# Attention stage: norm factors broadcast later in the first pair, value products of two units side by side in odd steps

## The chip, the cores and the metric

The kernel runs on one core of a Trainium2 chip. The metric is the device time of one execution in microseconds (us), lower is better. A core has TensorE (PE, matrix products, with its weight loads shown as PEld), VectorE (DVE), ScalarE (ACT), GpSimd (POOL) and SyncE (SP, which issues DMAs here). Each engine works through its own queue in order; semaphores tie them together.

## The reference

A decoder trunk of two layers on one sequence of 1024 positions and width 1024. Layer 0 mixes with an RG-LRU recurrence, layer 1 with stick-breaking attention; each is followed by a SwiGLU network. The change lies in the attention of layer 1, cut here to what matters (16 heads of 64; `hn` is the normed input):

```python
hn = rms_norm(h, mix_norm[1])
q, k, v = split(hn @ w_qkv)                 # 16 heads of 64 each
for blk in range(8):                        # 128 queries at a time
    z = (q_blk @ k[:t1].T) * scale
    strict = s_idx < t_idx
    log_fail = where(strict, log_sigmoid(-z), 0)
    suffix = reverse_cumsum(log_fail) - log_fail
    weights = where(strict, exp(log_sigmoid(z) + suffix), 0)
    out_blk = weights @ v[:t1]
h = h + concat(out_blks) @ w_o
```

## The kernel before

Products in nearly full precision are made from a high and a low part of each operand, three matmuls per product (`mm3`, lines 143 to 145), in f32 form with 512 columns. The value products (`av_part`, line 1802) are f16.

**Attention works on pairs of heads.** There are 8 pairs. Each pair needs its Q, K and V projections: `qkv_steps` makes them one after the other (`which` 0, 1, 2), each for two halves `n` of the positions, each half being 8 calls of `mm3`, one per call of the generator. So a half is 8 calls and a pair 48. After the eighth call of a half comes `evacuate`, in two parts: the first in the same call, the second at the start of the next call, before that call's products.

- Q: first part, ACT copies the rounded high part (L1660). Second part, DVE subtracts for the low part (L1651) and stages `spread` (ACT copies, L1648, and DMAs).
- K: first part, DVE multiplies the projection by the norm factors (L1665). Second part stages `high`, ACT's rounding copy (L1673), which stages `low` (DVE's subtraction, then `place`, ACT copies L1640 and DMAs), which stages the rest of `place`.
- V: first part, DVE scales (L1610); second part, DVE takes differences (L1612) and stages an ACT copy two steps later (L1627), then DVE's low part and transposing DMAs.

`stage` puts a task on a list; `due` runs it at the start of the next step (or a later one), ahead of everything else in that step. A second list, `later`, gives up one task per step: the splitting of the next projection's weights (`whi` on ACT, L1558, `wlo` on DVE, L1559), the squares of the weights (ACT, L1553), the column sums of these (PE, `n_ps`, L1537, followed by DVE at L1543) and the collecting of finished heads (`gather`, `add_v`, `parts`).

**The step loop.** One step `u` takes one chunk of scores and one unit of value products. Both lists have 192 entries, 24 per pair; the chunk is ten steps ahead of the unit. In a step the code issues, in this order: the staged tasks; loads of stored rows back to the chip; the scores (`z_part`, PE, L1690 and L1691, into one of two PSUM buffers that `n_ps` also uses), their sigmoid (ACT, L1728) and the scan (DVE, L1735 or L1738); for the chunk of the step before, ACT's cast (L1750), DVE's low part (L1751) and a transposing DMA; in even steps the value products of unit `u`; one task of `later`; two calls of the projections (`fill`); in odd steps the value products of unit `u`. In the last pair the weights are transposed on PE instead (`t_part`, `t_split`): even steps do this for the units `u+2` and `u+3`, after the value products of unit `u`.

The order written here is the order on each engine (`manual_schedule`), so an instruction that waits holds up all that stand behind it on its engine.

**The start.** 42 calls of the first pair's projections run before the step loop, numbered `i`. A table `between` puts other work after a call: `stats` (PE sums of squares, then the square root on ACT and small DVE operations that make the norm factors `rcol`) and `broadcast_r` (PE spreads the factors over all partitions, L192, and DVE copies them to `rbc`, L199). Call 17 begins the K projection, calls 24 and 32 end its halves, which read `rbc[0]` and `rbc[1]`. The column sums of the first pair come in call 22.

Of the kernel before, what the change touches and what calls it, by code (L numbers as in the profile page):

```python
# [34 lines left out]
def trunk(  # L35
# [152 lines left out]
    def broadcast_r(ps_pool, tag, n):  # L188
        ps = ps_pool.tile([P, NB], F32, tag=tag, name="rb_ps")
        for i in range(4):  # L190
            b = 4 * n + i
            nc.tensor.matmul(  # L192
                ps[:, i * P : (i + 1) * P],
                lhsT=rcol[:, b : b + 1].broadcast_to([P, P]),
                rhs=ident,
                start=True,
                stop=True,
            )
        nc.vector.tensor_copy(rbc[n], ps)  # L199
# [1288 lines left out]
    with ExitStack() as st:  # L1488
# [5 lines left out]
        psO = st.enter_context(tc.tile_pool(name="psO", bufs=2, space=PSUM, reuse_waits="tile"))  # L1494
# [25 lines left out]
        def stage(task, steps=1):  # L1520
            soon.append([steps, task])

        def load_link(i):
            q, which = divmod(i, 3)
            if q < NP:
                raws[i] = load_raw(cols(w_qkv, which * D + q * P), (ND,))
            else:
                mix[0].load(which)
# [233 lines left out]
        def unit_list(q, hx):  # L1762
            kbs = ((0, 1, 2, 3), (4, 5, 6, 7, 0, 1, 2, 3))
            return [(q, hx, G, kb, kb == 4 * G, kb == 3) for G in range(2) for kb in kbs[G]]
# [20 lines left out]
        def av_part(q, hx, G, kb, first, last):  # L1785
            q0 = (max(kb, 4 * G) - 4 * G) * P
            if first:
                av[0] = psO.tile([P, NB], F32, tag="o", name="av_ps")
            ps = av[0]
            k = kb % 4  # L1790
            parts_ = []
            if q == LAST:
                parts_ = [(q0, NB, t[:, q0:].rearrange("p (j c) -> p j c", c=P)) for t in ready.pop((hx, G, kb))]
            else:
                T_ = T[q, hx, G, kb // 4 == G]
                if kb // 4 == G and k < 2:
                    tp = T[q, hx, G, "pair"]
                    parts_ = [(q0, 2 * P, tp[:, x : x + 3 : 2] if k == 0 else tp[:, 4 + x : 5 + x]) for x in range(2)]
                c0 = max(q0, 2 * P) if kb // 4 == G else 0
                parts_ += [(c0, NB, T_[:, 2 * k + x, max(k - 2, 0) * (kb // 4 == G) :]) for x in range(2)]  # L1800
            for i, (c0, c1, t) in enumerate(parts_):
                nc.tensor.matmul(  # L1802
                    ps[:, c0:c1].rearrange("p (j c) -> p j c", c=P), lhsT=VV[q][:, hx, kb], rhs=t,
                    start=first and i == 0, stop=last and i == len(parts_) - 1,
                )
            if not last:
                return
            a, b = (top, bot)[:: 1 if hx == 0 else -1]

            def gather():  # L1810
                if hx == 0:
                    oo[q, G] = ap.tile([P, NB], F32, tag="oo", name="oo", bufs=2)
                o = oo[q, G]
                nc.scalar.copy(o[a], ps[b])
                nc.vector.tensor_add(o[a], ps[a], o[a])

            def add_v():
                eng = nc.vector if q == NP - 1 else nc.gpsimd
                eng.tensor_add(oo[q, G], oo[q, G], VT[q][:, G * NB + 1 : (G + 1) * NB + 1])

            def parts():
                o = oo[q, G]
                down = f32(av_[q])

                def both(hi, lo):
                    nc.scalar.activation(hi, o, AF.Copy, scale=down)
                    nc.vector.scalar_tensor_tensor(lo, o, down, f32(hi), op0=ALU.mult, op1=ALU.subtract)

                if not kept(q, G):
                    both(xh[q][G], xl[q][G])  # L1830
                else:
                    oh = ap.tile([P, NB], F32R, tag="oh", name="oh", bufs=1)
                    both(oh, o.bitcast(F32R))

                    def store():
                        nc.sync.dma_start(od[q, G][0], f32(oh))
                        nc.sync.dma_start(od[q, G][1], o)

                    stage(store)

            later.insert(0, gather)
            if hx == 1:
                later.extend((add_v, lambda: None, parts))
# [3 lines left out]
        units = [u for q, hx in heads for u in unit_list(q, hx)]  # L1847
# [27 lines left out]
        with tc.manual_schedule(engines={E.PE, E.Activation, E.DVE, E.Pool, E.SP}):  # L1875


            load_link(1)
            first = qkv_steps(0)
            between = {  # L1880
                12: lambda: stats(rbc[0], psO, "o", 0),
                16: lambda: stats(rbc[1], psO, "o", 1),
                17: lambda: broadcast_r(psO, "o", 0),
                18: lambda: nc.gpsimd.tensor_scalar_mul(rs, rcol, -SC),
                21: lambda: broadcast_r(psO, "o", 1),
            }
            def due():
                now = soon[:]
                soon.clear()
                for steps, task in now:  # L1890
                    if steps > 1:
                        stage(task, steps - 1)
                    else:
                        task()

            for i in range(1, 2 * ND * NH + 3 + AHEAD):
                next(first)
                if i in between:
                    between[i]()
                due()  # L1900
                if i > 4 and later:
                    later.pop(0)()

            gains = [len(units) - x for x in (31, 29, 27)]

            last_two, out_work = len(units) - 2 * 12, out_fill()
            amount = {x: 2 for x in (9, 10, 11, 12)}
            amount.update({x: 1 for x in (*range(-5, 1), *range(14, 21))})
            c = 0

            def turn(some):
                for a in some:
                    turn_weights(*a)

            for u in range(-LEAD, len(units)):
                some = chunks[c : c + 1]
                c += 1
                if u < -2:
                    for _ in range(2):
                        next(fill, None)  # L1920
                due()
                for _ in range(2 if u >= last_two - 8 and u % 2 == 0 else 1):
                    if back:
                        nc.sync.dma_start(*back.pop(0))
                for a in some:
                    z_rest(z_part(*a), *a)
                if u % 2 == 0 and u + 2 >= last_two:
                    av_part(*units[u])
                    two = [(x, t_part(*x)) for x in units[u + 2 : u + 4]]
                    for x, tp in two:  # L1930
                        ready[x[1:4]] = t_split(tp, *x)
                for a in some:
                    scan(*a)
                now, turning = turning, list(some)
                turn(now)
                if u % 2 == 0 and 0 <= u < last_two - 2:
                    av_part(*units[u])
                if u - last_two == 9:
                    mix[0].w[mix[0].order[1]] = next_weights(mix[0].raw.pop(1), nc.gpsimd)
                if later:  # L1940
                    later.pop(0)()
                if u >= -2:
                    for _ in range(2):
                        next(fill, None)
                for _ in range(amount.get(u - last_two, 0)):
                    next(out_work)
                if u in gains:
                    z_rest(z_part(*chunks[c]), *chunks[c])
                    scan(*chunks[c])
                    turning.append(chunks[c])  # L1950
                    c += 1
                if u % 2 and u >= 0:
                    av_part(*units[u])
            while later or soon:
                due()
                if later:
                    later.pop(0)()
# [46 lines left out]
```

## Time and profile before

| what | us |
|---|---|
| median of 3 runs | 2117.93 (2116.54 to 2119.25) |
| the profiled execution | 2116.7 |
| its span | 2114.9 |
| PE busy | 2096.8 |
| DVE busy | 1771.3 |
| ACT busy | 1184.5 |

The engine table gives busy time over the whole span, the windows give it for a stretch, with the granted TensorE clock (1.00 is full speed). A row of a timeline has the start, the duration, the engine, the line, the operation with what it writes and reads, a count, and in brackets the idle time before it with what ended that. The duration of a matmul reaches over its pipeline, so the distance of two starts tells what it costs the queue. The attention stage lies between about 953 and 1400 us of the span.

### The profile page before, as it was taken

The page shows a single profiled execution, that of the slowest core. Times are in us where ns is not written, and L with a number is a line of the kernel's source. Part 1 is how long each engine was busy: PE and PEld are TensorE (multiplying, and loading weights), DVE is VectorE, ACT ScalarE, POOL GpSimd, SP SyncE. Part 2 cuts the span into 40 slices and gives each one's busy share as a digit, 9 for nine tenths or more (in the row PEclk, how much of TensorE's full clock was granted, in tenths as well). Part 3 has the DMA queues.
Part 4 walks back from the last instruction along what each step waited for, and adds up shares of the span by engine and source line. Part 5 has one row for each costly group of instructions (what it writes and reads, how often), then busy time and mean ns, then how long its engine had stood idle before and what let it go on. Part 6 is the DMA issues. An engine that isn't in the chain of part 4 may idle for free.

```text
span 2114.9 us, 27976 instructions
## 1 busy us (share of the span) xinstructions
PE 2096.8 (99%) x10022; PEld 1719.9 (81%) x10022; DVE 1771.3 (84%) x2579; ACT 1184.5 (56%) x1906; POOL 139.1 (7%) x118
## 2 busy tenths in 40 slices
PE   8999999999999999999999999999999999999998
PEld 7888888888888888887777777678888888888887
DVE  7888778888888788796999999967888888888886
ACT  6567535444344445466878878744544444454456
POOL 1222010000000000000011111012000000000002
PEclk9999999999999999999999999999999999999999
DMA  7111431334444776533888898942224444686452
GB/s 240 50 50 40 149 100 55 105 124 145 161 133 152 256 251 190 152 118 91 162 179 175 177 178 174 247 170 80 85 90 150 140 150 155 202 269 225 126 153 90
DMA packets 446444, 313.89 MB, mean 148 GB/s; under 512 B 166104, under 2 KB 361824, under 8 KB 446304
## 3 DMA queue, kind: packets, MB, share of 16 engines
q1 hardware_dynamic: 446144, 311.84, 51.1%
q8 instruction: 78, 1.28, 0.3%
q14 instruction: 62, 0.51, 0.1%
q10 hardware_dynamic: 160, 0.27, 0.0%
HBM read 183.57 MB, written 82.84 MB: 126 GB/s over the span
## 4 chain that ended last, share of the span: by engine, by line
PE 93%; DVE 3%; ACT 1%; DMA 1%; issue 1%; SPq 0%; DVEq 0%; ACTq 0%
PE p_ps L143 18%; PE p_ps L145 18%; PE p_ps L144 18%; PE qk_ps L143 3%; PE qk_ps L145 3%; PE qk_ps L144 3%; PE a_ps L144 3%; PE a_ps L145 3%; PE a_ps L143 3%; PE ob_ps L143 3%; PE ob_ps L145 3%; PE ob_ps L144 3%; PE av_ps L1802 2%; PE i_ps L145 1%; PE i_ps L144 1%; PE i_ps L143 1%
## 5 line engine op out<-in xcount | busy, mean ns | idle before, releaser
L143 PE MATMUL p_ps<-vh,wbh 128*128 128x512 f32 x524 | 204.9, 391 | 0.0
L144 PE MATMUL p_ps<-vl,wbh 128*128 128x512 f32 x524 | 204.5, 390 | 0.0
L145 PE MATMUL p_ps<-vh,wbl 128*128 128x512 f32 x524 | 204.0, 389 | 0.2 <-DVE wbl L726 0.2
L143 PE MATMUL p_ps<-vh,wch 128*128 128x512 f32 x524 | 204.2, 390 | 0.0
L145 PE MATMUL p_ps<-vh,wcl 128*128 128x512 f32 x524 | 204.1, 389 | 0.0
L144 PE MATMUL p_ps<-vl,wch 128*128 128x512 f32 x524 | 203.9, 389 | 0.0
L722 ACT CAST wbh<-sb 128x1024 fp32r<-128x1024 f32 (+2 forms) x69 | 69.6, 1009 | 192.6 <-DVE sb L702 192.6
L145 PE MATMUL p_ps<-vh,wal 128*128 128x512 f32 x396 | 154.0, 389 | 0.0
L143 PE MATMUL p_ps<-vh,wah 128*128 128x512 f32 x396 | 154.0, 389 | 0.0
L144 PE MATMUL p_ps<-vl,wah 128*128 128x512 f32 x396 | 154.0, 389 | 0.0
L145 PEld LDWEIGHTS p_ps<-vh,wbl 128*128 128x128 f32 x524 | 98.4, 188 | 21.6 <-DVE wbl L726 0.7
L145 PEld LDWEIGHTS p_ps<-vh,wcl 128*128 128x128 f32 x524 | 98.4, 188 | 20.9 <-DVE wcl L736 0.6
L143 PEld LDWEIGHTS p_ps<-vh,wch 128*128 128x128 f32 x524 | 98.4, 188 | 20.5 <-ACT tb L1181 0.2
L144 PEld LDWEIGHTS p_ps<-vl,wch 128*128 128x128 f32 x524 | 98.3, 188 | 20.5
L143 PEld LDWEIGHTS p_ps<-vh,wbh 128*128 128x128 f32 x524 | 98.6, 188 | 19.8 <-ACT U L1181 0.4
L144 PEld LDWEIGHTS p_ps<-vl,wbh 128*128 128x128 f32 x524 | 98.6, 188 | 18.5
L143 PE MATMUL qk_ps<-vh,whi 128*128 128x512 f32 x264 | 113.2, 429 | 0.0
L1728 ACT ACTIVATE w<-z_ps,rs 128x512 f32<-128x512 f32 (+2 forms) x168 | 96.7, 579 | 15.1 <-PE z_ps L1691 12.0
L144 PE MATMUL qk_ps<-vl,whi 128*128 128x512 f32 x264 | 103.8, 393 | 0.0
L145 PE MATMUL qk_ps<-vh,wlo 128*128 128x512 f32 x264 | 103.7, 393 | 0.0
L1750 ACT CAST wx<-w 128x512 f16<-128x512 f32 (+1 forms) x140 | 80.1, 572 | 38.4 <-DVE w L1735 20.0
L1735 DVE TENSOR_TENSOR_SCAN w<-w,unit 128x128 f32<-128x128 f32 (+1 forms) x112 | 93.4, 834 | 9.5 <-ACT w L1728 8.3
(417 smaller groups left out, 5834.3 us busy)
## 6 DMA issues: line engine op xcount, KB each, us to landing
raw<-in_ffn_w_in SPq DMA_DIRECT2D x88, 512.0 KB, 4.0
vl<-pd SPq DMA_DIRECT2D x128, 256.0 KB, 3.6
pd<-U SPq DMA_DIRECT2D x90, 256.0 KB, 2.3
raw<-in_ffn_w_out SPq DMA_DIRECT2D x56, 256.0 KB, 3.6
raw<-in_attn_w_qkv SPq DMA_DIRECT2D x24, 512.0 KB, 4.2
h<-hd SPq DMA_DIRECT2D x32, 256.0 KB, 5.7
hd<-h SPq DMA_DIRECT2D x32, 256.0 KB, 2.0
g<-hd SPq DMA_DIRECT2D x32, 256.0 KB, 5.3
```

Of the source, the lines that this page charges most:

```text
L143: nc.tensor.matmul(ps, lhsT=wh, rhs=mh, start=first, stop=False, **kw)
L144: nc.tensor.matmul(ps, lhsT=wh, rhs=ml, start=False, stop=False, **kw)
L145: nc.tensor.matmul(ps, lhsT=wl, rhs=mh, start=False, stop=last, **kw)
L722: nc.scalar.copy(self.full(self.wb), self.full(self.sb))
L1728: nc.scalar.activation(F, ps[:, 0:n], AF.Sigmoid, scale=rs[:, j : j + 1])
L1735: nc.vector.tensor_tensor_scan(rev, rev, unit[:, NB - n :][:, ::-1], 0.0, op0=ALU.mult, op1=ALU.add)
L1750: nc.scalar.copy(wx[:, 0:m, 0], F)
L1802: nc.tensor.matmul(ps[:, c0:c1].rearrange("p (j c) -> p j c", c=P), lhsT=VV[q][:, hx, kb], rhs=t, start=first and i == 0, stop=last and i ...
```

## The change

The two broadcasts of the norm factors move from calls 17 and 21 to calls 22 and 25. In the step loop the value products of an even unit leave the even step and stand directly ahead of those of the odd unit, at the end of the odd step. The calls of the projections are divided anew: three in an even step and one in an odd step, in place of two and two.

```diff
             between = {
                 12: lambda: stats(rbc[0], psO, "o", 0),
                 16: lambda: stats(rbc[1], psO, "o", 1),
-                17: lambda: broadcast_r(psO, "o", 0),
                 18: lambda: nc.gpsimd.tensor_scalar_mul(rs, rcol, -SC),
-                21: lambda: broadcast_r(psO, "o", 1),
+                22: lambda: broadcast_r(psO, "o", 0),
+                25: lambda: broadcast_r(psO, "o", 1),
             }
...
                 if u % 2 == 0 and u + 2 >= last_two:
-                    av_part(*units[u])
                     two = [(x, t_part(*x)) for x in units[u + 2 : u + 4]]
...
-                if u % 2 == 0 and 0 <= u < last_two - 2:
-                    av_part(*units[u])
                 if u - last_two == 9:
...
                 if u >= -2:
-                    for _ in range(2):
+                    for _ in range(1 if u % 2 else 3):
                         next(fill, None)
...
                 if u % 2 and u >= 0:
+                    av_part(*units[u - 1])
                     av_part(*units[u])
```

## The prediction

> **What bounds the kernel now.** I read the page first (engine table, then the chain of waits), then busy time by stretches of the span, then the timelines of single engines. Units are us from the start of the span.
>
> ```profile
> PE 2096.8 (99%) x10022; PEld 1719.9 (81%) x10022; DVE 1771.3 (84%) x2579; ACT 1184.5 (56%) x1906; POOL 139.1 (7%) x118
> ...
> PE 93%; DVE 3%; ACT 1%; DMA 1%; issue 1%; SPq 0%; DVEq 0%; ACTq 0%
> ```
>
> TensorE (PE) is busy for 99% and carries 93% of the chain, so only what shortens PE's own queue or makes PE wait counts. The averages hide the attention stage, where the change lies. One stretch of it by windows (engines in the order PE, PEld, DVE, ACT, POOL, then the granted clock):
>
> ```profile
> 1100.00:1150.00 50.00, 50.00 (x262) 37.76 (x261) 48.16 (x69) 40.53 (x76) 5.72 (x7) 1.00 0.86 176
> ```
>
> PE never waits here, but VectorE (DVE) is busy 48.16 of 50 and ScalarE (ACT) 40.53. All three work through queues written in code order. PE is the bound with little behind it: if DVE and ACT come late at one place by more than PE's lead there, PE stops.
>
> The profiled execution took 2116.7 (span 2114.9 and 1.8 around it), 1.2 under the median of 2117.93. I sum the change against that execution and carry the sum to the median. 0.2%, about what a measurement can tell from no change, is 4.2 us.
>
> **Part 1: the two broadcasts.** PE's timeline at the start of attention, ACT's squares, and one window:
>
> ```profile
> 967.35 0.39 PE L144 MATMUL qk_ps<-vl,whi 128*128 128x512 f32 x1
> 967.58 0.39 PE L145 MATMUL qk_ps<-vh,wlo 128*128 128x512 f32 x1
> 969.88 1.13 PE L192 MATMUL rb_ps<-ident,rcol 128*128 128x128 f32 x8 [1.91 <-DVE rcol L183]
> ...
> 971.08 0.53 PE L144 MATMUL qk_ps<-xg,whi 128*128 128x512 f32 x1
> ...
> 974.72 0.39 PE L144 MATMUL qk_ps<-vl,whi 128*128 128x512 f32 x1
> ...
> 976.78 0.35 PE L1537 MATMUL n_ps<-g,sq 128*128 128x1 bf16 x8
> ```
> ```profile
> 971.68 1.15 ACT L1553 ACTIVATE sq<-raw 128x512 bf16<-128x512 f32 x2
> ```
> ```profile
> 972.00:973.00 1.00, 1.00 (x4) 0.81 (x3) 0.94 (x2) 0.82 (x2) 0.80 (x1) 0.50 0.74 166
> ```
>
> The first broadcast makes PE wait 1.91 for the norm factors. Afterwards the granted clock is 0.50 for a while: from 971.08 to 974.72 nine 512-column products start in 3.64, at full clock (0.23 apart, the first two rows) they take 2.07, so 1.57 is lost. Moved from call 17 to 22, the broadcast has 15 products ahead of it (3.4 us): PE arrives at about 967.8+3.4=971.2, when the factors are done (before 969.88). The wait goes, and with it what followed it. Next on PE now stand, directly behind the broadcast (0.97, from 969.88 to the 0.23 before 971.08), the column sums `n_ps`, which need the squares, done on ACT at 971.68+1.15=972.83. PE is there at 972.2 and waits 0.65. The copies of the factors (DVE) still precede the K products that read them. Sum: 1.91+1.57-0.65, a **gain of 2.9**; bounds 1.3 (the half clock comes all the same) to 3.5 (no new wait).
>
> **Part 2: value products side by side.** The products are the same, only their neighbours change. Two value products between f32 products, and six in a row near the end:
>
> ```profile
> 1105.38 0.61 PE L1802 MATMUL av_ps<-wt,v 128*128 128x512 f16 x2
> ...
> 1106.06 0.40 PE L144 MATMUL qk_ps<-vl,whi 128*128 128x512 f32 x1
> ```
> ```profile
> 1393.24 1.47 PE L1802 MATMUL av_ps<-wx,v 128*128 128x512 f16 x6
> ...
> 1394.79 0.40 PE L144 MATMUL ob<-vl,whi 128*128 128x512 f32 x1
> ```
>
> Each stretch ends with one f32 product (0.23), hidden by the left-out row. Two cost 0.68-0.23=0.45, 0.225 each; six cost 1.55-0.23=1.32, 0.220 each. Four in a row instead of twice two save about 0.02 to 0.03. With 96 pairs that is a **gain of 2.7** (bounds 0, if these rows differ by chance, to 5, if twice as much goes).
>
> **Part 3: the fill moved with them.** To make room, even steps now take three projection calls and odd steps one. A projection ends every eighth call, in an even step; its second half of evacuation comes with the next call, which was in the odd step and is now in the same even step. What that half stages runs one step earlier. For K: DVE's product with the norm factors (L1665) stays at the end of steps 4 and 8 of each cycle of 24, but ACT's rounding copy (L1673) moves from steps 6 and 10 to steps 5 and 9, ahead of the sigmoid (L1728) there. ACT then waits for DVE, which runs behind, and the sigmoid, the copies, the squares (L1553, steps 8 and 9) and PE's column sums (step 10) queue behind that wait. One cycle of before, steps 77 to 82, ACT, DVE and PE:
>
> ```profile
> 1171.28 0.69 ACT L1728 ACTIVATE w<-z_ps,rs 128x512 f32<-128x512 f32 x1
> 1171.87 0.50 ACT L1750 CAST wx<-w 128x384 f16<-128x384 f32 x1
> 1172.27 0.62 ACT L1558 CAST whi<-raw 128x512 fp32r<-128x512 f32 x1
> 1173.28 0.62 ACT L1673 CAST two<-two 128x512 fp32r<-128x512 f32 x1 [0.39 <-DVE two L1665]
> 1173.81 0.36 ACT L1728 ACTIVATE w<-z_ps,rs 128x128 f32<-128x128 f32 x1
> 1174.41 0.62 ACT L1750 CAST wx<-w 128x512 f16<-128x512 f32 x1 [0.24 <-DVE w L1735]
> ...
> 1176.72 0.47 ACT L1728 ACTIVATE w<-z_ps,rs 128x256 f32<-128x256 f32 x1
> 1177.10 1.24 ACT L1640 CAST kk<-two 64x512 fp32r<-64x512 f32 x2
> 1178.36 0.58 ACT L1728 ACTIVATE w<-z_ps,rs 128x384 f32<-128x384 f32 x1
> ...
> 1179.77 0.68 ACT L1728 ACTIVATE w<-z_ps,rs 128x512 f32<-128x512 f32 x1
> 1180.34 0.50 ACT L1750 CAST wx<-w 128x384 f16<-128x384 f32 x1
> 1180.74 0.63 ACT L1553 ACTIVATE sq<-raw 128x512 bf16<-128x512 f32 x1
> ```
> ```profile
> 1172.58 0.67 DVE L1665 TENSOR_TENSOR two<-qk_ps,rbc 128x512 f32<-128x512 f32 x1
> 1173.17 1.20 DVE L1735 TENSOR_TENSOR_SCAN w<-w,unit 128x512 f32<-128x512 f32 x1
> ...
> 1177.23 0.69 DVE L1735 TENSOR_TENSOR_SCAN w<-w,unit 128x256 f32<-128x256 f32 x1 [0.28 <-ACT w L1728]
> 1177.84 0.67 DVE L1559 TENSOR_TENSOR wlo<-raw,whi 128x512 fp32r<-128x512 f32 x1
> 1178.97 0.96 DVE L1735 TENSOR_TENSOR_SCAN w<-w,unit 128x384 f32<-128x384 f32 x1 [0.47 <-ACT w L1728]
> ...
> 1180.30 0.68 DVE L1665 TENSOR_TENSOR two<-qk_ps,rbc 128x512 f32<-128x512 f32 x1
> ```
> ```profile
> 1181.40 0.61 PE L1802 MATMUL av_ps<-wt,v 128*128 128x512 f16 x2
> 1181.84 0.34 PE L1537 MATMUL n_ps<-g,sq 128*128 128x1 bf16 x8
> ```
>
> Second K half alone: its product ends at 1180.30+0.68=1180.98. Now the copy waits for that (0.53 to the next instruction, as 1173.28 to 1173.81), then the sigmoid of step 81 (0.57), the cast (0.40), the second squares (0.63): squares done at 1183.11 instead of 1181.37. PE gets to the column sums at 1181.40, since the value products that stood there have moved behind: it waits **1.7**. That is the lower bound.
>
> The first K half adds to it. Its copy still starts at 1173.28, but the three ACT instructions that ran before it (1171.28 up to 1172.27 and its 0.53: 1.5) now stand behind it. The sigmoid of step 77 ends at about 1174.5, and the scan that began at 1173.17 begins 1.3 later. ACT has one pause of 0.24 up to the sigmoid of step 79, and one pair of K copies more ahead of that (1177.10 to 1178.36: 1.26). So that sigmoid starts near 1176.72+1.5+1.26-0.24=1179.24 and ends at 1179.7; its scan and the `wlo` behind it take 1.2, the scan of step 80 starts near 1180.9 instead of 1178.97, and the second K product, 1.33 after it, near 1182.25. That is 1.95 late, and the wait on PE becomes 1.7+1.95=**3.65**, the upper bound. I take 3.3, near the upper bound, because these rows leave ACT only 0.24 to absorb anything, less a little because PE's stop lets DVE catch up. This holds for the six cycles of pairs 2 to 7. In the cycle of pair 1 the squares come at steps 5 and 6 and the sums at step 7, so only the first K half is in the way: between 0 and 3.3, I take 2. **Loss: 6x3.3+2=21.8.**
>
> The other halves are hidden. Q's subtraction on DVE needs ACT's copy, which ends before DVE gets there; V's second half keeps its distance of two steps. The last uses of the projection inputs come up to one step earlier, so SP's loads back also do, which costs nothing.
>
> **Part 4: the clock after these waits.** Part 1 showed 1.57 lost at half clock after a wait of 1.91. Seven waits of 2 to 3.3 can each be followed by the same; a wait split over two of whatever periods the clock is judged by may escape. I take five of seven: **loss 7.9**, bounds 0 and 11. [...]
>
> **Part 5: the end of attention.**
>
> ```profile
> 1350.00:1357.00 7.00, 5.26 (x25) 3.55 (x26) 6.97 (x10) 4.07 (x8) 1.09 (x1) 1.00 0.92 237
> 1357.00:1381.00 24.00, 22.38 (x130) 15.85 (x129) 23.91 (x34) 16.63 (x33) 4.36 (x3) 1.00 0.68 214
> ```
>
> PE idles 1.74+1.62=3.36 here while DVE is full. If PE was held up in step 154, DVE has less behind it when PE arrives: I take half, a **gain of 1.7** (0 to 3.4).
>
> **Sum:** -2.9-2.7+21.8+7.9-1.7=+22.4, on 2116.7 it is 2139.1, on the median 2140.3. I say **2140**.
>
> **Rivals.**
> - *The waits come, the clock stays full.* 22.4-7.9=+14.5: 2132. For it: half clock appears after only one place of this trace's attention stage. Against it: that place waited less. [...] Chance 0.18.
> - *Only the second K half counts, clock full.* 7x1.7=11.9 instead of 21.8+7.9, the rest as above: +4.6, 2122.5. It needs DVE to lose the carry of the first half on the way; two DVE pauses (0.28, 0.47) are all that speaks for it. Chance 0.08.
> - *Faster: PE's lead hides the later squares.* Were DVE's K product done when ACT reaches its copy, ACT would not stop, and only parts 1 and 2 would remain: -5.6, 2112. The deciding point is DVE's lag: the product would have to end before about 1179.8 (the first squares' end), 1.2 sooner than at 1180.98. Against it: the 0.39 pause of ACT at 1173.28 shows that it waits for this product even a step later. Chance 0.10.
> - *The parts cancel* (about 0.8 per cycle): 2118, chance 0.04.
>
> **How the numbers follow.** The forecast has 0.60. Its own bounds are 2130 (short waits, two slow stretches) and 2149 (7 waits of 3.65, seven slow stretches, no gain at the end). The range 2121 to 2150 leaves out the last two rivals, 0.14. Faster 0.10, same 0.04, slower 0.86.
>
> **What the changed profile would show.** Right: `n_ps` on PE waits for ACT's `sq` seven times, 2 to 3.5 each; ACT's L1673 waits for L1665 over 1 us at a time; stretches of clock 0.50 inside the 50 us windows; no 1.91 at `rb_ps`, but some 0.6 at the first `n_ps`. Wrong: PE full from 1010 to 1350 with `n_ps` unbroken, which would mean that DVE's lag was smaller in the new order than these rows say.

## The result, and the profile after

The changed kernel is slower: 2145.62 us median (2144.06 to 2148.49, 4 runs) against 2117.23 (2115.86 to 2119.25, 4 runs) beside it, a ratio of 1.0138 with an interval of 1.0126 to 1.0150. The prediction was 2140 in 2121 to 2150. The profiled execution after is the slowest of the four, 2148.49, with a span of 2146.7: 31.8 longer than the one before, where the medians differ by 28.4.

The engine table and the chain after, and the same stretch of 50 us as before (PE, PEld, DVE, ACT, POOL, clock):

```profile
PE 2110.9 (98%) x10022; PEld 1735.1 (81%) x10022; DVE 1770.0 (82%) x2579; ACT 1187.1 (55%) x1906; POOL 133.9 (6%) x118
...
PE 85%; DVE 6%; issue 4%; ACT 4%; DMA 1%; POOL 0%; SPq 0%; DVEq 0%; POOLq 0%; ACTq 0%
...
1100.00:1150.00 50.00, 47.03 (x244) 35.91 (x242) 44.12 (x64) 39.05 (x72) 5.48 (x7) 1.00 0.82 172
```

The instruction counts are unchanged, and DVE and ACT work as much as before. PE, which never paused in this stretch, is now idle for 3 of 50 us and gets 244 matmuls done in place of 262; DVE, ACT and "issue" (time in which an engine waited for nothing that the profile shows) stand in the chain where PE stood. So it is order, not work. The waits of the attention stage (950 to 1430) say which order:

```profile
ACT two L1673 <- DVE two L1665: 30.4, 16, 2.9
...
PE n_ps L1537 <- ACT w L1728: 11.5, 7, 1.7
...
PE n_ps L1537 <- ACT sq L1553: 5.2, 8, 0.8
...
PE z_ps L1690 <- ACT w L1728: 4.4, 6, 0.9
```

Each line has who waits and for whom, the us in total, the times and the longest. The kernel before has for the copy (950 to 1400), and as the only wait listed for PE between 1008 and 1350:

```profile
ACT two L1673 <- DVE two L1665: 11.2, 9, 6.5
...
PE z_ps L1690 <- ACT wd L1728: 0.2, 1, 0.2
```

K's rounding copy on ACT now waits for DVE's K product all 16 times. The longest waits of both kernels lie in the first pair, whose copies come before the step loop (2.9 after, 6.5 before). In pairs 2 to 7 the copies of a cycle (the 24 steps of one pair) wait 2.0 and 1.5, where before the longest was 0.4. PE stands at the column sums seven times up to 1.7 and eight times up to 0.8, and six times 0.6 to 0.9 at scores. One cycle on ACT, DVE and PE:

```profile
1183.68 0.62 ACT L1673 CAST two<-two 128x512 fp32r<-128x512 f32 x1 [2.04 <-DVE two L1665]
...
1193.40 0.62 ACT L1673 CAST two<-two 128x512 fp32r<-128x512 f32 x1 [1.46 <-DVE two L1665]
1193.93 0.68 ACT L1728 ACTIVATE w<-z_ps,rs 128x512 f32<-128x512 f32 x1
1194.51 0.50 ACT L1750 CAST wx<-w 128x384 f16<-128x384 f32 x1
1194.91 0.63 ACT L1553 ACTIVATE sq<-raw 128x512 bf16<-128x512 f32 x1
```
```profile
1192.69 0.68 DVE L1665 TENSOR_TENSOR two<-qk_ps,rbc 128x512 f32<-128x512 f32 x1
1194.64 1.23 DVE L1735 TENSOR_TENSOR_SCAN w<-w,unit 128x512 f32<-128x512 f32 x1 [1.27 <-ACT w L1728]
```
```profile
1187.52 0.45 PE L1690 MATMUL z_ps<-kk,q 128*128 128x384 f32 x1 [0.91 <-ACT w L1728]
...
1192.58 0.39 PE L1691 MATMUL z_ps<-kk,q 128*128 128x512 f32 x1
1194.66 0.24 PE L1537 MATMUL n_ps<-g,sq 128*128 128x1 bf16 x4 [1.69 <-ACT w L1728]
1195.60 0.25 PE L1537 MATMUL n_ps<-g,sq 128*128 128x1 bf16 x4 [0.69 <-ACT sq L1553]
1195.71 0.47 PE L143 MATMUL qk_ps<-vh,whi 128*128 128x512 f32 x1
```

The K product ends at 1193.37 and the copy starts at 1193.40; sigmoid, cast and squares follow without a gap, which is the chain of the prediction. PE is released in two pieces: `n_ps` writes into a buffer of the scores, which the sigmoid must have read (1.69), then its second half needs the second squares (0.69). With the 0.91 ahead of a score product, that is 3.3 in this cycle; it is 3.0 in those where that last wait is shorter.

The spans in parts, by the starts of matmuls that both traces have (the n-th score product):

| stretch | before | after | change | of it half clock |
|---|---|---|---|---|
| first product of `stats` to 1st scores | 29.43 | 26.39 | -3.0 | |
| 11th to 35th (cycle of pair 1) | 50.62 | 54.39 | +3.8 | 1.7 |
| 35th to 155th (five cycles) | 253.83 | 277.73 | +23.9 | 6.5 |
| 155th to 168th (the sixth cycle's sums) | 28.02 | 34.65 | +6.6 | 3.1 |
| 168th to the last | 35.67 | 35.46 | -0.2 | |

The rest is the same within 0.03, and 0.76 lies ahead of the first mark. The last column is an estimate: half of PE's busy time in the stretches at a granted clock of 0.50, where f32 products of 512 columns start 0.43 apart (after, 1086.41 to 1088.54), against 0.23 at a clock of 1.00 (1089.72 and 1089.95). There are three stretches of 3.41 and two of 6.83, seven times 3.41 in all. One with the time before it, a place without half clock, and one of the long ones:

```profile
1082.24:1085.65 3.41, 1.02 (x12) 0.60 (x11) 2.14 (x4) 2.43 (x5) 0.00 (x0) 1.00 0.36 76
1085.65:1089.06 3.41, 3.41 (x10) 2.63 (x10) 2.91 (x6) 3.15 (x6) 0.00 (x0) 0.50 0.86 214
...
1191.47:1194.88 3.41, 1.72 (x11) 0.93 (x10) 2.14 (x4) 1.95 (x4) 0.00 (x0) 1.00 0.40 77
1194.88:1198.29 3.41, 2.71 (x16) 2.27 (x16) 2.90 (x4) 3.37 (x7) 0.00 (x0) 1.00 0.78 200
...
1249.49:1256.32 6.83, 6.28 (x19) 4.60 (x20) 4.32 (x8) 5.01 (x9) 0.48 (x3) 0.50 0.80 182
```

The first and the third row are windows with the waits of one cycle. In the first PE is busy for 1.02, and half clock follows; in the third it is busy for 1.72, and none follows.

The start of attention after:

```profile
971.96 1.05 PE L192 MATMUL rb_ps<-ident,rcol 128*128 128x128 f32 x8
973.16 0.24 PE L1537 MATMUL n_ps<-g,sq 128*128 128x1 bf16 x4
973.64 0.25 PE L1537 MATMUL n_ps<-g,sq 128*128 128x1 bf16 x4 [0.24 <-ACT sq L1553]
```

The wait of 1.91 at `rb_ps` and the half clock behind it are gone. The half clock is not sure to follow that wait, though. The kernels with the division alone and with K's copy alone (below) leave the broadcasts where they were and wait the same 1.92 there; no half clock follows in their traces, and the stretch to the first scores takes 27.85 in both, in place of 29.43.

### The profile page after: what moved, and what is told of

Read it like the earlier page. It is cut to its first block, busy times and chain, and to the rows that moved or that the text cites. A ratio compares the mean times of both kernels' runs of the same rounds, so it can differ in the third digit from the quotient of the medians.

```text
span 2146.7 us, 27992 instructions
## 1 busy us (share of the span) xinstructions
PE 2110.9 (98%) x10022; PEld 1735.1 (81%) x10022; DVE 1770.0 (82%) x2579; ACT 1187.1 (55%) x1906; POOL 133.9 (6%) x118
## 4 chain that ended last, share of the span: by engine, by line
PE 85%; DVE 6%; issue 4%; ACT 4%; DMA 1%; POOL 0%; SPq 0%; DVEq 0%; POOLq 0%; ACTq 0%
PE p_ps L143 18%; PE p_ps L145 18%; PE p_ps L144 18%; PE a_ps L144 3%; PE a_ps L145 3%; PE a_ps L143 3%; PE ob_ps L145 3%; PE ob_ps L144 3%; PE ob_ps L143 3%; PE qk_ps L143 2%; PE qk_ps L144 2%; PE qk_ps L145 2%; PE i_ps L145 1%; PE i_ps L144 1%; PE i_ps L143 1%
## 5 line engine op out<-in xcount | busy, mean ns | idle before, releaser
L143 PE MATMUL qk_ps<-vh,whi 128*128 128x512 f32 x264 | 106.4, 403 | 0.0
L143 PE MATMUL p_ps<-vh,wd 128*128 128x512 f32 x254 | 99.4, 391 | 0.0
```

The source lines that it names most:

```text
L143: nc.tensor.matmul(ps, lhsT=wh, rhs=mh, start=first, stop=False, **kw)
```

## The experiments

The theory is the prediction's part 3: K's rounding copy, which comes a step earlier because a projection's last call and the next call now share an even step, stops ACT. The rival is that the new order itself does it: value products at the end of odd steps, three calls on end in even ones. Besides, each part of the change was tried by itself.

**The copy put back.** The changed kernel, with K's copy at its old step in pairs 1 to 7:

```diff
-                stage(high)
+                stage(high, 2 if q else 1)
```

> The changed kernel, but K's rounding copy on ACT is staged two steps after the call that issues it instead of one, so that it stands in steps 6 and 10 of a cycle again; all else of the change stays. Theory 1 (the copy that moved ahead blocks ACT, and through it PE): the waits at the column sums and the slow clock go, parts 1 and 2 of the sum remain, 2112 (2110 to 2115), faster than before by 0.1 to 0.35%. Theory 2 (the new order on PE itself, value products side by side with the scores of odd steps later, makes ACT and DVE late): the waits stay, over 2135.

Measured: 2118.11 (11 runs), ratio 1.0007 (0.9998 to 1.0016). One line takes nearly all of the loss away (1.5 is left over the 2116.57 of the kernel before, run beside it), and the stretch of 1100 to 1150 is nearly whole again:

```profile
1100.00:1150.00 50.00, 49.62 (x260) 38.20 (x259) 46.92 (x69) 40.27 (x75) 5.73 (x7) 1.00 0.83 174
```

The theory holds and the rival falls. The expected gain over the kernel before is missing, though: the start gives 3.1, but the five cycles take 255.37 in place of 253.83, and in the last pair a wait of PE grows from 0.67 to 1.93. ACT, then PE:

```profile
1351.93 0.63 ACT L1627 ACTIVATE vx<-t 128x512 f16<-128x512 f32 x1 [2.37 <-DVE t L1612]
```
```profile
1353.09 0.68 PE L1690 MATMUL z_ps<-kk,q 128*128 128x512 f32 x1 [1.93 <-ACT wd L1728]
```

V's staged copy, one step earlier too, waits for DVE just as K's did. The prediction had called V's half hidden.

**Parts of the change alone**, on the kernel before. The division of the calls:

```diff
-                    for _ in range(2):
+                    for _ in range(1 if u % 2 else 3):
```

> The kernel before with one edit alone: three projection calls in even steps, one in odd steps. Value products and broadcasts stay where they were. Theory 1: slow by the K copy; the value products ahead of the column sums hide 0.45 of each wait, 6x2.9+2 = 19 and 5 to 7 stretches of half clock, 2140 to 2148. Theory 2: the value products have not moved, so no change, 2115 to 2120.

Measured: 2146.39 (4 runs), ratio 1.0136 (1.0122 to 1.0150). The whole loss comes with this line. At the column sums of one cycle:

```profile
1195.24 0.61 PE L1802 MATMUL av_ps<-wt,v 128*128 128x512 f16 x2
1197.34 0.24 PE L1537 MATMUL n_ps<-g,sq 128*128 128x1 bf16 x4 [1.48 <-ACT w L1728]
1198.27 0.25 PE L1537 MATMUL n_ps<-g,sq 128*128 128x1 bf16 x4 [0.69 <-ACT sq L1553]
```

Here the value products still stand ahead of the sums, and PE waits only 0.2 less for that, not the expected 0.45: what PE does earlier or later around this place counts for little, since ACT and DVE set the pace of the cycle. Off the five cycles (274.07, with 3.3 of half clock) the loss is 3.4 per cycle, beside 3.5 in the changed kernel.

The K copy alone, nothing else moved (the copy staged one step earlier, before the generator's pause, for `q` over 0):

```diff
-                yield
-                stage(high)
+                if q:
+                    stage(high)
+                yield
+                if not q:
+                    stage(high)
```

> The kernel before with one edit: from the second pair on, K's rounding copy on ACT is staged with the first half of the evacuation, so it stands in steps 5 and 9 of a cycle instead of 6 and 10. Calls, value products, Q, V, weights and broadcasts stay. Theory 1: this alone makes the waits at the column sums, 3.4 less 0.45 hidden by the value products, times six, 2 for the first cycle, and 3 to 7 stretches of half clock at 1.7: 2117+20+8 = 2145 (2137 to 2150). Rival (the weights, loads and Q's and V's halves that moved with it make up half or more of the loss): under 2132.

Measured: 2142.81 (4 runs), ratio 1.0124 (1.0110 to 1.0138). It is the same wait with calls and value products where they were. The five cycles take 273.87; without three stretches of 3.41 at half clock (1.7 each) that is a loss of 3.0 per cycle, of the changed kernel's 3.5. PE's waits between 1000 and 1380 (in this kernel the sigmoid is L1731):

```profile
PE n_ps L1537 <- ACT w L1731: 6.8, 7, 1.0
PE n_ps L1537 <- ACT sq L1553: 4.5, 7, 0.7
```

The value products side by side, with two calls in each step:

```diff
-                    av_part(*units[u])
...
-                if u % 2 == 0 and 0 <= u < last_two - 2:
-                    av_part(*units[u])
...
                 if u % 2 and u >= 0:
+                    av_part(*units[u - 1])
                     av_part(*units[u])
```

> The kernel before with the value products of both units at the end of the odd step, projection calls two and two, broadcasts where they were. Theory 1: no K copy moves, so the gain of part 2 alone, 2114.5 (2112 to 2117.5). Theory 2: slow, over 2125.

Measured: 2119.30 (11 runs), ratio 1.0010 (1.0001 to 1.0019): the expected gain is not there. Its trace has two reasons. With the value products gone from ahead of them, the column sums come 0.45 earlier, on the heels of the squares:

```profile
1182.61 0.58 PE L1690 MATMUL z_ps<-kk,q 128*128 128x512 f32 x1
1183.04 0.39 PE L1691 MATMUL z_ps<-kk,q 128*128 128x512 f32 x1
1183.27 0.63 PE L1537 MATMUL n_ps<-g,sq 128*128 128x1 bf16 x8
1183.76 0.47 PE L143 MATMUL qk_ps<-vh,whi 128*128 128x512 f32 x1
```

From their start to the next product they take 0.49; the last experiment below has 0.21 for the same without a wait. The five cycles take 254.17, 0.3 more than before and 1.9 more than in that experiment.

The other reason is larger in this trace, and lies in the last pair: from the 168th scores on it takes 39.41 in place of 35.67. PE waits there for a stored row that SP loads back; this trace, then before:

```profile
1360.22 0.51 PE L144 MATMUL ob<-vl,whi 128*128 128x512 f32 x1 [2.51 <-DMA vl<-odl]
```
```profile
1356.53 0.50 PE L144 MATMUL ob<-vl,whi 128*128 128x512 f32 x1 [1.07 <-DMA vl<-odl]
```

Half clock follows the wait of 2.51 at 1360.87 (mean granted clock of this execution 0.998, of the one before 0.999). This execution is the slowest of the eleven, so how much of this the median holds is open.

The broadcasts alone, at calls 22 and 25:

> The kernel before with the broadcasts at calls 22 and 25 alone. Both theories: the gain of part 1, 2114.3 (2113.7 to 2116); if the half clock comes at that place for another reason than the wait, only 1.3 is gained, 2116.

Measured: 2114.44 (11 runs) beside 2116.57, ratio 0.9987 (0.9978 to 0.9996). From the first product of `stats` to the first scores it takes 26.38, 3.05 less than before. At calls 20 and 22 instead:

> The kernel before with the broadcasts at calls 20 and 22 alone. PE reaches call 20 at about 967.8+2.0=969.9, when the first factors are just done, and passes the column sums after both broadcasts, when the squares are done: the gain of e4 and 0.6 more, 2113.7 (2112.8 to 2115). If the first factors come later than PE, a wait of some tenths takes that back, 2114.5.

Measured: 2114.18 (11 runs), ratio 0.9991 (0.9982 to 0.9999). No wait is left at the first sums, the stretch takes 25.81; in the medians the two cannot be told apart.

**All of the change with the copies kept**: K's copy at its old step, V's too, broadcasts at 20 and 22.

> The changed kernel with K's and V's staged ACT copies put back to the steps they had before (K two steps after, V one step more than now) and the broadcasts at calls 20 and 22, ahead of the first column sums instead of around them. Theory 1 (staged ACT copies that wait for DVE are all that costs): the 0.65 of the first column sums goes, the wait of 1.9 at the end of attention that e1 showed goes, 2113 (2111 to 2116). Rival (value products side by side cost something of their own in the middle): 2117 and over, with 1 or more lost between steps 24 and 144.

Measured: 2116.75 (11 runs), ratio 1.0000 (0.9991 to 1.0009), a miss. The five cycles take 255.16, 1.3 more than before: the gain of the start is given back in small pieces all along the cycles. Short waits of the column sums for the squares, as with the value products alone, are a part of them (0.9 in three places); the rest was not taken apart. V's part is shown: its copy no longer waits in the last pair, and PE's wait there is 0.67 again, as before.

**The half clock.** The changed kernel with eight spare products of 512 columns ahead of the column sums of pairs 1 to 7, into a buffer that nothing reads:

```diff
+                if q:
+                    spare = psT.tile([P, NB], F32, tag="T", name="spare_ps")
+                    for _ in range(8):
+                        nc.tensor.matmul(spare, lhsT=xh[7][0][:, 0:P], rhs=xh[7][0], start=True, stop=True)
```

> The changed kernel with eight more products of 512 columns on PE ahead of the column sums of pairs 2 to 8, into a PSUM tile that nothing reads: 1.84 of PE work per cycle that falls into the wait. If the half clock follows from PE's idle time there, it goes at most places, and the kernel with more work is faster than the changed one by 7 to 12: 2134 to 2139. If the half clock has another cause, 2145 or more.

Measured: 2140.15 (4 runs), ratio 1.0112 (1.0098 to 1.0126), just above the expectation. PE does more work, and the kernel is 5.5 us faster than the changed one:

```profile
1189.80 2.02 PE L1538 MATMUL spare_ps<-vh 128*128 128x512 f32 x8
1191.66 0.25 PE L1541 MATMUL n_ps<-g,sq 128*128 128x1 bf16 x4
1192.59 0.25 PE L1541 MATMUL n_ps<-g,sq 128*128 128x1 bf16 x4 [0.68 <-ACT sq L1557]
```

In this kernel the sums are L1541 and the squares L1557. The spare products lie in the wait of 1.69, and nothing from 1010 to 1400 is at half clock (the granted clock is 1.00 in each 50 us). So the half clock of the changed kernel came with PE's idle time at the sums: with the longest wait of a cycle filled, it is gone. The five cycles, 272.43, are 3.7 each above before, without any half clock: that is the loss by the waits and by what fills one of them, alone.

**One half of K at a time.** The changed kernel with only the second copy early (`stage(high, 2 if q and n == 0 else 1)`), then with only the first (`n == 1`):

> The changed kernel, but of K's two rounding copies in pairs 1 to 7 only the second runs a step earlier, the first stays where it was. By the prediction's working the second half alone makes PE wait 1.7 us at the column sums in each of six cycles and nothing in the first pair's: the version with both copies kept (2118.1) plus 10.2 is 2128.3 us, and up to 2138 if each wait of 1.7 us is followed by half clock (1.7 more). Rival, only both copies together overload ACT and DVE: 2118 to 2121 us.

> The changed kernel, but of K's two rounding copies in pairs 1 to 7 only the first runs a step earlier. By the prediction's working this holds up the scans and with them the second K product by 1.95 us and the squares by about as much; the second copy, a step later than in the changed kernel, has room for that, so PE waits some 1.5 us at the column sums in seven cycles: 2118.1+10.5=2128.6 us, up to 2138 with half clock. Rival, the first half's delay is caught up before the squares: 2118 to 2121 us, and the whole of the loss is the second half's.

Measured: 2130.88 (4 runs), ratio 1.0065 (1.0050 to 1.0081), and 2131.36 (4 runs), ratio 1.0067 (1.0053 to 1.0080). In both the first expectation holds for the time, with some half clock. The five cycles take 266.89 and 263.37. Off 253.83, and with three stretches of 3.41 at half clock (1.7 each) taken from the first, that is 1.6 and 1.9 per cycle. Together they make 3.5, what both cost in the changed kernel. Off the 255.37 of the kernel with both copies put back, which differs from these by the copies alone, it is 1.3 and 1.6, together 2.9 of 3.2. The place is not the expected one for the first copy: in pairs 2 to 7 it makes PE wait 0.4 at the sums, not 1.5, and up to 0.9 at scores (second of these kernels, 1000 to 1380):

```profile
PE z_ps L1690 <- ACT w L1728: 4.8, 6, 0.9
PE n_ps L1537 <- ACT sq L1553: 3.5, 7, 0.8
```

Windows of the first of these kernels, two with the waits of a cycle, each with the one that follows:

```profile
1185.61:1189.02 3.41, 1.64 (x14) 1.09 (x14) 2.14 (x4) 3.15 (x6) 0.00 (x0) 1.00 0.55 134
1189.02:1192.43 3.41, 3.41 (x10) 2.64 (x9) 2.44 (x5) 2.44 (x5) 0.19 (x1) 0.50 0.87 202
1240.22:1243.64 3.42, 2.08 (x16) 1.69 (x16) 2.29 (x4) 3.38 (x8) 0.00 (x0) 1.00 0.82 206
1243.64:1247.05 3.41, 3.41 (x17) 2.38 (x16) 3.12 (x5) 3.36 (x7) 1.05 (x2) 1.00 0.85 159
```

The first window holds 1.77 of idle time, and half clock follows; the third row holds 1.34, and none follows.

**Value products side by side, with the sums out of their way.** The kernel before with broadcasts at 20 and 22, the value products of pairs 0 to 6 side by side, two calls in each step, and the column sums a step later:

```diff
-                stage(factors, 2)
+                stage(factors, 1 if q else 2)
...
-            return lambda: squared(0), lambda: squared(1), sums
+            wait = (lambda: None,) if q else ()
+            return lambda: squared(0), lambda: squared(1), *wait, sums
...
-                if u % 2 == 0 and 0 <= u < last_two - 2:
-                    av_part(*units[u])
...
                 if u % 2 and u >= 0:
+                    if u < last_two - 2:
+                        av_part(*units[u - 1])
                     av_part(*units[u])
```

> The kernel before with the norm factors' broadcasts after calls 20 and 22, value products side by side in odd steps for pairs 0 to 6 (the last pair keeps its order), two projection calls in every step, and the column sums of pairs 1 to 7 one step later, with what they feed at the same step as before. With the pairs alone, PE's value products of five cycles took 1.2 us less and its column sums waited 2.1 us more for the squares. If the waits for the squares are what the pairs lost, they go: from step 24 to step 144 PE needs 253.8-1.2=252.6 us and the time is 2114.2-1.7=2112.5 us. Rival, the pairs save nothing on PE whatever stands beside them: 253.8 us for that stretch and 2114.2 us.

Measured: 2112.22 (11 runs) beside 2117.82, ratio 0.9976 (0.9967 to 0.9985). It is faster than both kernels. The sums no longer wait, and the window is full:

```profile
1179.44 0.40 PE L1692 MATMUL z_ps<-kk,q 128*128 128x512 f32 x1
1179.68 0.35 PE L1537 MATMUL n_ps<-g,sq 128*128 128x1 bf16 x8
1179.89 0.48 PE L143 MATMUL qk_ps<-vh,whi 128*128 128x512 f32 x1
```
```profile
1100.00:1150.00 50.00, 50.00 (x263) 38.80 (x263) 48.68 (x71) 41.03 (x77) 5.44 (x7) 1.00 0.92 179
```

The five cycles take 252.23, 1.60 less than with the broadcasts alone (253.83): 0.027 for each of the 60 odd steps in which the products of two units now stand together.

## Why the prediction was right, and what its sum missed

- **Part 3, right.** The waits came at the column sums, for the reason named: K's copy alone makes them, and putting it back takes them away. 3.3 per cycle were taken; the five cycles show (23.9-6.5)/5=3.5, the sixth 6.6-3.1=3.5, the cycle of pair 1 3.8-1.7=2.1 (2 taken). The lower bound of 1.7 (second half) and the 1.95 that the first half adds were each found alone, as 1.6 and 1.9, or 1.3 and 1.6 off the kernel with the copies put back. Two details differ. No single wait has the forecast 2 to 3.5: PE is released at the sums first by the sigmoid (it must have read their buffer), after 1.7, and for the last 0.7 by the squares. And 0.6 to 0.9 of the loss lies at the scores, where the first half's delay shows.
- **Part 1, right, with luck in it.** 2.9 predicted, 3.0 in the trace; the broadcasts alone gave 2.1 by the medians and 2.8 by the ratio. Of this the 1.57 of half clock was taken as sure, but in two of the four traces with the broadcasts at calls 17 and 21 it did not come after the same wait; the waits alone give 27.85-26.39=1.5. The new wait at the sums was 0.65 by the prediction; the trace has 0.24 ahead of the second half of the sums and about 0.2 ahead of the first (973.16 less 971.96 and the 0.97 that a broadcast takes).
- **Part 2, mis-sized.** A gain of 2.7 was summed, and in the changed kernel it is nil. The price of a pair was right (0.028 said, 0.027 measured); the step that failed is that it was summed as if PE set the pace there. Alone it was lost at the column sums, which need something on PE between them and the squares, and in the last pair at the loads; in the changed kernel, with ACT and DVE setting the pace, it only makes PE wait longer (1.69 beside 1.48). Without half clock the five cycles take 271.2 there, and 270.8 with the division alone.
- **Part 4, too small.** 7.9 was taken, five times 1.57. The trace has half clock in five stretches, seven times 3.41 in all, 11.3 by half of their busy time, a little over the bound of 11: two of the stretches lasted 6.83, which had not been thought of. The waits here, none over 1.69 in one piece, brought half clock, and filling the longest took it away. One way to escape that the part names is seen: in the cycle of the third row above PE is idle for 2.39, 1.69 of it ahead of 1194.88 and 0.70 behind, and no half clock follows; in the first row the 2.39 lie together, and it does.
- **Part 5, wrong.** The gain of 1.7 at the end did not come: the stretch from the 168th scores on is 0.2 shorter. DVE is full there in both kernels, and PE idles 3.2 in place of 3.6. That the same stop held up DVE too, so that it brought no lead along, is likely, but was not tried by itself (after, then before):

```profile
1372.41:1407.88 35.47, 32.30 (x183) 23.39 (x181) 35.17 (x52) 24.47 (x47) 3.49 (x3) 1.00 0.80 223
```
```profile
1340.41:1376.08 35.67, 32.12 (x181) 23.00 (x180) 35.51 (x51) 24.90 (x49) 3.01 (x3) 1.00 0.96 260
```

Together 2.7 (pairs), 3.4 (clock), 1.5 (end) and 1.2 (waits), less 0.1 in part 1, make the 8.7 between the predicted +22.4 and the +31.1 of the table. These four all lie on one side, so no errors cancelled; the waits of part 3, nearly right in size, carry the forecast. The median of after is 2.9 below its profiled execution, so 2140 was 5.6 low. The forecast's lower end of 2130 is not worked out in the prediction: seven waits of 1.7 and two slow stretches of 1.57, with parts 1, 2 and 5 as summed, make +7.7, which is 2125.7 on the median. The rivals with full clock, with one K half, with a hidden wait, and with parts that cancel are out: each is contradicted by a line above.

## What to carry to other kernels

Where several engines are nearly full and each works in code order, look for every staged task that a re-division of steps moves, not only the ones that the change names: one copy that comes a step earlier than its producer can deliver stops its engine for everybody behind it (K's copy alone: 2142.81 us beside 2116.63). A saving on the busiest engine counts only where that engine still sets the pace; give its neighbours a step's distance first, then the saving shows (the pairs of value products: 2119.30 us alone, 2112.22 with the sums a step later and the broadcasts moved). In the changed kernel the five stretches at half clock each came behind 3.41 us in which PE had been idle for 1.75 to 2.39, and they cost, by the estimate above, 11.3 on top of the waits; eight spare products (2.02) in the longest wait made it 5.5 us faster, so such a wait is worth filling.

## What the runs showed of the hardware

In the trace of the changed kernel five stretches of the attention stage are at a granted clock of 0.50. They start at 1024.21, 1085.65, 1249.49, 1307.52 and 1362.13, which are 18, 48, 17 and 16 times 3.413 us apart, and last 3.41 (three) or 6.83 (two). The table counts pieces of 3.41 us from the start of a stretch, over the whole stage in the first two kernels, in six and three pieces that hold waits in the other two. It gives PE's idle time in a piece at full clock, by the clock of the piece that comes next:

| kernel | us idle, next at 0.50 | us idle, next at 1.00 |
|---|---|---|
| before | 1.91 | at most 1.07 |
| changed | 2.13, 2.39, 1.83, 2.39, 1.75 | 1.69, 1.69, the rest at most 1.05 |
| only the second copy early | 1.85, 1.77, 1.75 | 1.43, 1.34, 0.95 |
| only the first copy early | 1.89, 1.92 | 0.91 |

So half clock came behind pieces in which PE was still busy for up to 1.66 of the 3.41. No rule follows from these rows: with the division alone and with K's copy alone none came behind the wait of 1.92 at the first broadcast, and with K's copy alone it came in the cycles behind single waits of at most 1.0. What decides was not shown. The two stretches of 6.83 in the changed kernel have PE idle for 0.55 and 0.64 in their first 3.41, the three of 3.41 for at most 0.05.

The five cycles took 253.83 with the broadcasts alone and 252.23 with the f16 value products of two units next to each other as well, 0.027 us less for each of the 60 places (the column sums moved by a step as well).
